# A pooling kernel that streams 168 MB: 840 columns moved into a first piece on 120 partitions, and the last sums done by pairwise adds

## The chip, the cores and the metric

The kernel runs on one core of one Trainium2 chip. The metric is the device time of one execution in microseconds. A run counts as fast when it is within 1.5% of the fastest of the same kernel.

## The reference

The input is 32 x 256 x 4096 fp32, p is 2 and the window is 4. Every four neighbours along the last axis become one output.

```python
window = np.abs(x[:, :, start:end]) ** p
result[:, :, i] = (np.mean(window, axis=-1)) ** (1.0 / p)
```

So each output is the root of a quarter of a sum of four squares. 134.22 MB are read and 33.55 MB are written, and every element is touched once.

## The kernel before

The flat input is treated as 128 partitions of 262,144 columns. SyncE issues the loads, most of them 13,184 columns wide, into three rotating input tiles. ScalarE squares in place, VectorE sums groups of four with a reduce, ScalarE takes the root one chunk later, and ScalarE issues a store for every two loads. The last four stores are issued by SyncE, behind all loads.

```python
    W, O_W = 13184, 6592
    X_SLOTS, O_SLOTS = 3, 2
    slots = [[(W, [4416, 4384, 4384])]] * 18
    slots += [[(6592, [3296, 3296])] * 2, [(6592, [3296, 3296]), (5056, [2528, 2528])]]
    groups = [2] * 9 + [3, 1]
    late = {7, 8, 9, 10}
    # ... cut ...
        for step in chunks:
            v = xs[i][:, c:c + step]
            nc.scalar.activation(out=v, in_=v, func=Act.Square)
            o = ots[g][:, at + c // k:at + (c + step) // k]
            nc.vector.tensor_reduce(
                out=o, in_=v.rearrange("p (n j) -> p n j", j=k),
                axis=mybir.AxisListType.X, op=mybir.AluOpType.add,
            )
            if pending is not None:
                root(*pending)
            # ... cut ...
    root(*pending)
    for g in sorted(late):
        store(g, nc.sync)
```

Of the kernel before, what the change touches and what calls it, by code (L numbers as in the profile page):

```python
# [1 line left out]

# [4 lines left out]


@with_exitstack
def kernel(  # L10
    ctx: ExitStack,
    tc: tile.TileContext,
    x: bass.AP,
    p: float,
    kernel_size: int,
    out: bass.AP,
):






    nc = tc.nc

    assert float(p) == 2.0, "kernel specialized for p == 2"
    k = int(kernel_size)
    assert k == 4, "kernel specialized for kernel_size == 4"

    P = nc.NUM_PARTITIONS  # L30
    fp32 = mybir.dt.float32
    Act = mybir.ActivationFunctionType
    xf = x.rearrange("b c l -> (b c l)")
    of = out.rearrange("b c l -> (b c l)")
    total = xf.shape[0] // P

    W, O_W = 13184, 6592
    X_SLOTS, O_SLOTS = 3, 2
    slots = [[(W, [4416, 4384, 4384])]] * 18
    slots += [[(6592, [3296, 3296])] * 2, [(6592, [3296, 3296]), (5056, [2528, 2528])]]  # L40
    groups = [2] * 9 + [3, 1]
    late = {7, 8, 9, 10}
    in_x = {9, 10}


    loads = [(s, sum(w for w, _ in slot[:j]), *slot[j]) for s, slot in enumerate(slots)
             for j in range(len(slot))]
    n = len(loads)
    assert sum(w for _, _, w, _ in loads) == total

    firsts = [sum(groups[:g]) for g in range(len(groups))]
    assert sum(groups) == n
    group_of = [g for g, count in enumerate(groups) for _ in range(count)]
    columns = [sum(w for _, _, w, _ in loads[firsts[g]:firsts[g] + groups[g]])
               for g in range(len(groups))]

    x_pool = ctx.enter_context(tc.tile_pool(name="x_pool", bufs=X_SLOTS))
    o_pool = ctx.enter_context(tc.tile_pool(name="o_pool", bufs=O_SLOTS))
    ctx.enter_context(tc.manual_schedule())

    def block(flat, g, div):
        at, width = sum(columns[:g]) * P // div, columns[g] * P // div
        return flat[at:at + width].rearrange("(p w) -> p w", p=P)

    slot_tiles = {}
    xs = {}

    def load(i):
        s, at, w, _ = loads[i]
        if at == 0:  # L70
            slot_tiles[s] = x_pool.tile([P, W], fp32, name="xt")
        v = slot_tiles[s][:, at:at + w]
        g = group_of[i]
        src = sum(loads[j][2] for j in range(firsts[g], i))
        nc.sync.dma_start(out=v, in_=block(xf, g, 1)[:, src:src + w])  # L75
        xs[i] = v

    ots = {}

    def store(g, queue):  # L80
        queue.dma_start(out=block(of, g, k), in_=ots[g])  # L81

    def root(g, o, ends):
        nc.scalar.activation(out=o, in_=o, func=Act.Sqrt, scale=1.0 / k)  # L84
        if ends and g not in late:
            store(g, nc.scalar)

    ahead = 0
    while ahead < n and loads[ahead][0] < X_SLOTS - 1:
        load(ahead)  # L90
        ahead += 1
    pending = None
    for i in range(n):
        s, _, w, chunks = loads[i]
        while ahead < n and loads[ahead][0] < s + X_SLOTS:
            load(ahead)
            ahead += 1
        g = group_of[i]
        if i == firsts[g]:
            pool, width = (o_pool, O_W) if g not in in_x else (x_pool, W)  # L100
            t = pool.tile([P, width], fp32, name="ot" if g not in in_x else "xt")
            ots[g] = t[:, 0:columns[g] // k]
        at = sum(loads[j][2] for j in range(firsts[g], i)) // k
        assert sum(chunks) == w
        c = 0
        for step in chunks:
            v = xs[i][:, c:c + step]
            nc.scalar.activation(out=v, in_=v, func=Act.Square)  # L108
            o = ots[g][:, at + c // k:at + (c + step) // k]
            nc.vector.tensor_reduce(  # L110
                out=o, in_=v.rearrange("p (n j) -> p n j", j=k),
                axis=mybir.AxisListType.X, op=mybir.AluOpType.add,
            )
            if pending is not None:
                root(*pending)
            c += step
            pending = (g, o, i == firsts[g] + groups[g] - 1 and c == w)
    root(*pending)
    for g in sorted(late):
        store(g, nc.sync)  # L120


# [1 line left out]
_INS = ['x', 'p', 'kernel_size']  # L124
_OUTS = [((32, 256, 1024), 'float32')]

_NUMBERS = {'p': 2.0, 'kernel_size': 4}


# [26 lines left out]
```

## Time and profile before

| what | value |
|---|---|
| time, median of the first three runs | 394.69 us (394.66 to 394.81) |
| span of the profiled run | 393.0 us |
| VectorE and ScalarE busy | 282.4 and 292.4 us |
| packets of the two data queues | 99.3% of sixteen DMA engines' span |
| last root begins, last store lands, end of the span | 386.42, 392.2, 393.0 us |

The prediction below shows the lines that carry this.

The trace records every DMA packet with its start, duration, size and queue, but not the engine. A packet is here one partition's row of a transfer: 13,184 columns of 4 bytes are 52,736 bytes. An engine's packets can still be chained, because each one starts 4 ns before the recorded end of the one before it. The *excess* is the sum over the 52,736-byte packets of their duration beyond the usual 1947 ns, divided by 16. *Lateness* is how long after the median one the last of the sixteen parts of a transfer lands (the page counts 528 packets under 512 bytes, all of 4 bytes in the records: sixteen for each of the 33 transfers). The *dip* is the stretch of slow packets when the first large store starts.

### The profile page before, as it was taken

To read this page: it belongs to the slowest core of one execution; us is meant where nothing else is said; L and a number is where in the kernel's file an instruction comes from. 1 tells how busy PE (TensorE), PEld (TensorE's weight loads), DVE (VectorE), ACT (ScalarE), POOL (GpSimd) and SP (SyncE) were. 2 spreads that over 40 slices of the span, in tenths; PEclk is the share of its full clock that TensorE was granted. 3 is DMA by queue.
4 is the path that set the end of the run, shared out by engine and by line. 5 is a ranking of instruction groups with operands and counts; after the bars stand their busy time and mean duration, and the time that the engine had idled before them with its cause. 6 is when DMAs were issued, how large, how long until landed. Compare 5 with 4: busy or idle time off the path is not lost.

```text
span 393.0 us, 316 instructions
## 1 busy us (share of the span) xinstructions
DVE 282.4 (72%) x62; ACT 292.4 (74%) x126; POOL 0.2 (0%) x4
## 2 busy tenths in 40 slices
DVE  0068989494959495949594959595859686899992
ACT  1099986777786768686958695959595949899991
POOL 0000000000000000000000000000000000000000
DMA  8999999999999999999999999999999999999997
GB/s 344 429 429 440 429 424 381 443 459 429 413 440 435 429 427 432 429 440 441 437 448 421 432 462 435 392 429 472 429 413 451 425 429 429 424 429 427 438 429 329
DMA packets 4754, 167.79 MB, mean 427 GB/s; under 512 B 528, under 2 KB 528, under 8 KB 656
## 3 DMA queue, kind: packets, MB, share of 16 engines
q1 hardware_dynamic: 3744, 144.15, 85.3%
q10 hardware_dynamic: 1008, 23.63, 14.0%
q14 instruction: 2, 0.02, 0.0%
HBM read 134.22 MB, written 33.55 MB: 427 GB/s over the span
## 4 chain that ended last, share of the span: by engine, by line
DMA 62%; ACT 19%; DVE 14%; issue 2%; ACTq 0%; SPq 0%
DMA xt<-in_x_dram 62%; ACT xt L108 15%; DVE ot L110 11%; DVE xt L110 3%; ACT ot L84 3%; ACT xt L84 1%; ACTq L81 0%; SPq L75 0%; ACTq L108 0%
## 5 line engine op out<-in xcount | busy, mean ns | idle before, releaser
L110 DVE TENSOR_REDUCE ot<-xt 128x1096 f32<-128x4384 f32 (+1 forms) x54 | 255.4, 4731 | 102.7 <-ACT xt L108 102.4
L108 ACT ACTIVATE xt<-xt 128x4384 f32<-128x4384 f32 (+3 forms) x62 | 230.3, 3716 | 89.2 <-DMA xt<-in_x_dram 86.3
L84 ACT ACTIVATE ot<-ot 128x1096 f32<-128x1096 f32 (+1 forms) x54 | 59.8, 1108 | 1.8 <-DVE ot L110 0.9
L110 DVE TENSOR_REDUCE xt<-xt 128x824 f32<-128x3296 f32 (+1 forms) x8 | 27.0, 3384 | 1.3 <-ACT xt L108 1.2
L84 ACT ACTIVATE xt<-xt 128x824 f32<-128x824 f32 (+1 forms) x8 | 6.7, 841 | 3.0 <-DVE xt L110 2.9
L108 ACT ACT_TABLE_LOAD x1 | 1.3, 1283 | 0.7 <-PEq L137 0.7
L84 ACT ACT_TABLE_LOAD x1 | 1.3, 1283 | 0.0
L137 POOL MEMSET const-bfloat16-1.0<- 128x1 bf16 x1 | 0.1, 101 | 0.0
L137 POOL MEMSET const-uint8-127<- 128x1 uint8 x1 | 0.1, 101 | 0.0
L137 POOL MEMSET const-float32-0.0<- 128x1 f32 x1 | 0.1, 98 | 0.2 <-issue 0.2
L137 POOL MEMSET const-float32-1.0<- 128x1 f32 x1 | 0.1, 98 | 0.0
## 6 DMA issues: line engine op xcount, KB each, us to landing
xt<-in_x_dram SPq DMA_DIRECT2D x18, 6592.0 KB, 39.7
out_dram<-ot ACTq DMA_DIRECT2D x7, 3296.0 KB, 26.4
xt<-in_x_dram SPq DMA_DIRECT2D x3, 3296.0 KB, 24.6
out_dram<-ot SPq DMA_DIRECT2D x2, 3296.0 KB, 29.6
xt<-in_x_dram SPq DMA_DIRECT2D x1, 2528.0 KB, 26.4
out_dram<-xt SPq DMA_DIRECT2D x1, 2472.0 KB, 9.3
out_dram<-xt SPq DMA_DIRECT2D x1, 632.0 KB, 5.0
```

Source lines behind the costliest of these rows:

```text
L84: nc.scalar.activation(out=o, in_=o, func=Act.Sqrt, scale=1.0 / k)
L108: nc.scalar.activation(out=v, in_=v, func=Act.Square)
L110: nc.vector.tensor_reduce(out=o, in_=v.rearrange("p (n j) -> p n j", j=k), axis=mybir.AxisListType.X, op=mybir.AluOpType.add,)
L137: nc = _bacc.Bacc("TRN2", target_bir_lowering=False, num_devices=1)
```

## The change

It has two parts. 840 columns are taken from the last load and laid as 120 rows of 896 floats, with a load, a square, a reduce, a root and a store of their own, ahead of everything else. From the seventeenth load on, two adds (first two pairwise sums of each four, then their sum) take the place of the reduce. The rotating tiles also become fixed ones.

```diff
-    slots += [[(6592, [3296, 3296])] * 2, [(6592, [3296, 3296]), (5056, [2528, 2528])]]
+    slots += [[(6592, [3296, 3296])] * 2, [(6592, [3296, 3296]), (4216, [2112, 2104])]]
+    ODD = 840
 ... cut ...
+    PAIRS = 16
 ... cut ...
+        q = v.rearrange("p (n j) -> p n j", j=k)
+        front = v[:, 0:v.shape[1] // 2]
+        h = front.rearrange("p (n j) -> p n j", j=2)
+        nc.vector.tensor_tensor(out=h, in0=q[:, :, 0:2], in1=q[:, :, 2:4], op=add)
+        nc.vector.tensor_tensor(out=o, in0=h[:, :, 0], in1=h[:, :, 1], op=add)
 ... cut ...
+    Q = 120
+    odd = ODD * P // Q
+    t = o_tiles[1][0:Q, 0:odd]
+    nc.sync.dma_start(out=t, in_=xf[(total - ODD) * P:total * P].rearrange("(p w) -> p w", p=Q))
     ahead = 0
 ... cut: the loads of the first three slots ...
+    nc.scalar.activation(out=t, in_=t, func=Act.Square)
+    o = o_tiles[1][0:Q, odd:odd + odd // k]
 ... cut: its reduce ...
+    nc.scalar.activation(out=o, in_=o, func=Act.Sqrt, scale=1.0 / k)
+    nc.scalar.dma_start(
+        out=of[(total - ODD) * P // k:total * P // k].rearrange("(p w) -> p w", p=Q), in_=o,
+    )
```

120 rows look like a wish to use fifteen DMA engines and to spare one for 1.24 us of work. The adds should shorten the compute after the last load.

More of the change, by code (lines that the diff above doesn't have):

```diff
@@ L39 @@
     slots = [[(W, [4416, 4384, 4384])]] * 18
-    slots += [[(6592, [3296, 3296])] * 2, [(6592, [3296, 3296]), (5056, [2528, 2528])]]
+    slots += [[(6592, [3296, 3296])] * 2, [(6592, [3296, 3296]), (4216, [2112, 2104])]]
+    ODD = 840
     groups = [2] * 9 + [3, 1]
     late = {7, 8, 9, 10}
-    in_x = {9, 10}
+    in_x = {9: (2, 0), 10: (2, 4944)}
+    FINE, ENDS, LAG = range(22), (), 1
+    PAIRS = 16
     loads = [(s, sum(w for w, _ in slot[:j]), *slot[j]) for s, slot in enumerate(slots)
@@ L48 @@
     n = len(loads)
-    assert sum(w for _, _, w, _ in loads) == total
+    assert sum(w for _, _, w, _ in loads) + ODD == total
     firsts = [sum(groups[:g]) for g in range(len(groups))]
@@ L55 @@
                for g in range(len(groups))]
-    x_pool = ctx.enter_context(tc.tile_pool(name="x_pool", bufs=X_SLOTS))
-    o_pool = ctx.enter_context(tc.tile_pool(name="o_pool", bufs=O_SLOTS))
+    x_pool = ctx.enter_context(tc.tile_pool(name="x_pool", bufs=1))
+    o_pool = ctx.enter_context(tc.tile_pool(name="o_pool", bufs=1))
+    x_tiles = [x_pool.tile([P, W], fp32, name=f"xt{j}") for j in range(X_SLOTS)]
+    o_tiles = [o_pool.tile([P, O_W], fp32, name=f"ot{j}") for j in range(O_SLOTS)]
     ctx.enter_context(tc.manual_schedule())
@@ L63, in block @@
         return flat[at:at + width].rearrange("(p w) -> p w", p=P)
-    slot_tiles = {}
     xs = {}
@@ L69, in load @@
         s, at, w, _ = loads[i]
-        if at == 0:
-            slot_tiles[s] = x_pool.tile([P, W], fp32, name="xt")
-        v = slot_tiles[s][:, at:at + w]
+        v = x_tiles[s % X_SLOTS][:, at:at + w]
         g = group_of[i]
@@ L86, in root, with total_sum @@
             store(g, nc.scalar)
+    def total_sum(o, v, i):
+        add = mybir.AluOpType.add
+        if i < PAIRS:
+            nc.vector.tensor_reduce(
+                out=o, in_=v.rearrange("p (n j) -> p n j", j=k),
+                axis=mybir.AxisListType.X, op=add,
+            )
+            return
+        q = v.rearrange("p (n j) -> p n j", j=k)
[7 more added lines that the diff above has]
+    nc.sync.dma_start(out=t, in_=xf[(total - ODD) * P:total * P].rearrange("(p w) -> p w", p=Q))
     ahead = 0
-    while ahead < n and loads[ahead][0] < X_SLOTS - 1:
+    while ahead < n and loads[ahead][0] < X_SLOTS:
         load(ahead)
         ahead += 1
-    pending = None
+    nc.scalar.activation(out=t, in_=t, func=Act.Square)
+    o = o_tiles[1][0:Q, odd:odd + odd // k]
+    nc.vector.tensor_reduce(
+        out=o, in_=t.rearrange("p (n j) -> p n j", j=k),
+        axis=mybir.AxisListType.X, op=mybir.AluOpType.add,
+    )
+    nc.scalar.activation(out=o, in_=o, func=Act.Sqrt, scale=1.0 / k)
+    nc.scalar.dma_start(
+        out=of[(total - ODD) * P // k:total * P // k].rearrange("(p w) -> p w", p=Q), in_=o,
+    )
+    pending = []
+    done = 0
     for i in range(n):
@@ L99 @@
         if i == firsts[g]:
-            pool, width = (o_pool, O_W) if g not in in_x else (x_pool, W)
-            t = pool.tile([P, width], fp32, name="ot" if g not in in_x else "xt")
-            ots[g] = t[:, 0:columns[g] // k]
-        at = sum(loads[j][2] for j in range(firsts[g], i)) // k
+            t, first = (o_tiles[g % O_SLOTS], 0) if g not in in_x else (x_tiles[in_x[g][0]], in_x[g][1])
+            ots[g] = t[:, first:first + columns[g] // k]
+            summed = rooted = 0
         assert sum(chunks) == w
@@ L108 @@
             nc.scalar.activation(out=v, in_=v, func=Act.Square)
-            o = ots[g][:, at + c // k:at + (c + step) // k]
-            nc.vector.tensor_reduce(
-                out=o, in_=v.rearrange("p (n j) -> p n j", j=k),
-                axis=mybir.AxisListType.X, op=mybir.AluOpType.add,
-            )
-            if pending is not None:
-                root(*pending)
-            c += step
-            pending = (g, o, i == firsts[g] + groups[g] - 1 and c == w)
-    root(*pending)
+            total_sum(ots[g][:, summed:summed + step // k], v, i)
+            while pending and pending[0][0] <= done - LAG:
+                root(*pending.pop(0)[1:])
+            done += 1
+            c += step
+            summed += step // k
+            ends = summed == columns[g] // k
+            if ends or i in FINE or (i in ENDS and c == w):
+                pending.append((done - 1, g, ots[g][:, rooted:summed], ends))
+                rooted = summed
+    for job in pending:
+        root(*job[1:])
     for g in sorted(late):
```

## The prediction

> **What bounds the kernel now.** I read the page first (busy shares, slices, queues), then the chain of waits, then a table of windows, and at the end the single DMA packets that the trace records.
>
> ```profile
> span 393.0 us, 316 instructions
> DVE 282.4 (72%) x62; ACT 292.4 (74%) x126; POOL 0.2 (0%) x4
> DMA  8999999999999999999999999999999999999997
> ...
> q1 hardware_dynamic: 3744, 144.15, 85.3%
> q10 hardware_dynamic: 1008, 23.63, 14.0%
> ```
>
> No compute engine is full, but the DMA row is at 9 in every slice but the first and the last, and the packets of the two data queues take 85.3 + 14.0 = 99.3% of sixteen engines' span. That leaves 0.7% of 393 us, 2.75 us, idle per engine. The window table tells where (columns: window, length, DVE busy, ACT busy, POOL busy, clock, DMA share, GB/s):
>
> ```profile
> 0.00:1.70 1.70, 0.00 (x0) 0.98 (x1) 0.20 (x4) 1.00 0.00 0
> 1.70:4.00 2.30, 0.00 (x0) 0.31 (x1) 0.00 (x0) 1.00 1.13 367
> 4.00:40.00 36.00, 15.09 (x4) 19.69 (x9) 0.00 (x0) 1.00 1.03 444
> 40.00:56.00 16.00, 14.60 (x4) 14.50 (x6) 0.00 (x0) 1.00 0.99 422
> 56.00:62.00 6.00, 5.44 (x2) 5.96 (x3) 0.00 (x0) 1.00 0.94 334
> 62.00:70.00 8.00, 7.36 (x2) 3.77 (x2) 0.00 (x0) 1.00 0.99 428
> 70.00:383.00 313.00, 236.95 (x52) 245.31 (x105) 0.00 (x0) 1.00 1.00 433
> ```
>
> Nothing moves for 1.7 us (the first load is issued at 0.73 us), then 433 GB/s nearly to the end. The one dip is 334 GB/s at 56 to 62 us, when the first output store, issued by ScalarE at 55.62 us, starts. It costs (433 - 334) x 6 us = 594 KB, or 1.4 us.
>
> The chain of waits could mislead (shares by engine):
>
> ```profile
> DMA 62%; ACT 19%; DVE 14%; issue 2%; ACTq 0%; SPq 0%
> ```
>
> and its last pieces, in order of time (start, length, what):
>
> ```profile
> 380.48 0.89 ACT xt L84
> 381.37 2.21 ACT xt L108
> 383.57 0.02 issue
> 383.60 2.80 DVE xt L110
> 386.39 0.02 issue
> 386.42 0.73 ACT xt L84
> ```
>
> It ends with square (L108), sum (L110), root (L84), and then the last store. From 339.7 us on, ScalarE is nearly full. Does that tail hold the end? The last store is issued at 387.15 us; issue to first packet was 1.0 us for the first load (0.73 to 1.74), so its packets could have begun at about 388.2. The packet records show them beginning at 389.2, each engine's following the 19,776-byte packets of the store before almost without a gap. So the tail has about 1.0 us of slack, and the DMA engines set the time: the last packet ends at 391.71, lands at 392.2, and the kernel ends at 393.0.
>
> Packet costs, from the same records: 52,736 bytes take 1947 ns, 26,368 take 978, 5,056 take 194. The line through the first two is 9 ns + 0.03675 ns per byte and gives 195 for the third. In undisturbed packets one engine's sixteenth is (2304 x 1947 + 1536 x 978 + 128 x (754 + 735 + 194)) / 16 ns = 387.7 us; 1.9 us to begin, about 0.65 us of slow first packets and some 1.3 us of slow packets near the first store make 391.5. Fifteen engines start their first packet between 1.74 and 2.28 us, one not before 3.19, so about 1.25 us late. At the end it (or whichever is last) is only 0.145 us behind the next (391.71 against 391.57): in this run the other engines lost their lead in the dip.
>
> [...]
>
> **The change part by part.**
>
> 1. Small piece, DMA engines. 840 columns leave the last 128-row load and store and come as 120 rows of 896 floats. Bytes are the same in total. Taken away per engine: 8 rows x (3360 + 840 bytes) x 0.03675 ns = 1.24 us. Added on fifteen engines: 8 x (9 + 3584 x 0.03675) = 1.13 us for the load and 8 x (9 + 896 x 0.03675) = 0.34 us for the store. Net +0.23 us on fifteen engines, -1.24 us on the spared one. That 1.24 equals the late engine's 1.25 us is surely the intent. I take the spared engine to be the late one; the trace does not number them. The kernel ends with its latest engine, now the next in line: -0.145 + 0.23 = +0.09 us.
>
> 2. Small piece, first use of the store queue. A 430 KB load landing near 4.5 us, its square (0.93 us[...]), reduce (1.09), a table load (1.28, under the reduce) and root (0.37) put the first ScalarE-issued store at about 7 us, on fifteen engines, instead of at 55.6. If the dip of 1.4 us belongs to the first use of that queue, it moves there; with only 107 KB it may shrink. If it belongs to the first large store, it stays. I give shrinking some 35% and about 1 us of gain: -0.35 us in the mean.
>
> 3. First loads. Three slots are asked for at once instead of two and one more directly after: before, the third was already issued ahead of any wait, so nothing moves. The small load delays the large ones by one issue (about 0.4 us), under which fifteen engines have 1.13 us of small rows: 0, or +0.1 on the spared engine.
>
> 4. Pairwise adds from load 16 on: 14 reduces become 28 adds. For 4384 columns [...]3.74 us replaces 4.72; for 3296, 2.89 replaces 3.59; for the last chunk (2104, was 2528), 1.96 replaces 2.78. VectorE loses 6 x 0.98 + 6 x 0.70 + 2 x 0.82 = 11.7 us of busy time. On the tail's path the gain is smaller, as ScalarE paces it: its waits of 0.94 and 0.67 us for VectorE go, the last two squares lose 0.35 us each, two roots 0.1 each, the last sum 0.84: 3.3 us. The last store is issued at about 384 instead of 387.15. All of it goes into slack, which grows from 1.0 to about 4 us, because the engines are still busy with the store before.
>
> 5. Fixed tiles in place of rotating ones, output groups 9 and 10 together in the third input tile: the instruction order of the SyncE loads and stores is otherwise the same, slots are reused as before, and I see no new wait. 0.
>
> Sum: +0.09 - 0.35 + 0.05 = -0.2 us. I predict **394.4 us**, after adding a further -0.1 for unprofiled runs in which the late engine may trail by more than the 0.145 us of this one profile.
>
> **Rivals.** (a) *The tail is the bound*: then part 4 gives 2 to 3 us, about 392 us. For it: the chain ends there, ScalarE is full from 339.7. Against it: the last store's packets queue behind others without a gap. (b) *The late engine is the bound and the dip shrinks*: the dip is what hid its lateness. If it shrinks, the ordinary engines end near 390.7 and sparing the late one is worth its whole 1.2 us: about 393.4. For it: the equality of 1.24 and 1.25. Against it: nothing shows that the dip depends on a first use. (c) *The small piece hurts*: small packets, or a wrong engine spared (the late one then carries +0.23), or a second dip: 394.9 to 396. (d) *The adds are slower[...]*, as the strided reads might make them: if they took twice as long, 5.8 us per 3296 columns against ScalarE's 3.7, VectorE would pace the tail and ten microseconds would be added. [...]I give this 1%.
>
> **Range and chances.** The terms are tenths of a microsecond, and repeats differ by 0.15 us; (b) and (c) span 393.4 to 395. Eight in ten: 393.2 to 395.1. Two per cent is 7.9 us, more than all idle time of the DMA engines (2.75 us) and the dip (1.4 us) together, so faster by over 2% is out of reach; slower needs rival (d).
>
> **What would show it.** Right: adds near 1.87 and 1.02 us for 3296 columns; VectorE's busy time about 10.6 us lower (11.7 less the small reduce); the last root near 384 us and yet the last landing within 1 us of 392.2; DMA share at 1.00 through the tail; the small load and store in fifteen parts. Wrong: DMA slices under 9 in the middle (a new wait for a slot), a dip at 56 to 62 us gone or doubled, a last store whose packets begin only after a gap, or a start later than 1.74 us.

The sum has lost no term: +0.09 - 0.35 + 0.05 is -0.21 us, and with the further -0.1 the 394.69 us of the kernel before become 394.4. But two of its grounds only the changed kernel's trace shows:

- *Fifteen engines, eight rows each*, on which the +0.09 rests. No transfer of 120 rows was in the trace before, whose 33 transfers of 128 rows have 528 packets of 4 bytes, sixteen each. The changed kernel has two transfers more and 558, fifteen for each of the two; the fifteen chains of the small load are described below.
- *The costs of the single instructions.* The adds for 4384, 3296 and 2104 columns took 2442 + 1300, 1875 + 1016 and 1255 + 707 ns, the 3.74, 2.89 and 1.96 us of the fourth point. The small piece's square, reduce, table load and root took 0.95, 1.09, 1.28 and 0.39 us.

The trace before did show that loads and stores take turns on an engine: beside the first large store (55.6 us on), a chain of packets goes 52,736 bytes, 26,368, 52,736, 26,368. Its stores take 26.2 us in the median to land and 33.7 at most, although none has more than 3.4 MB, about 8 us at 433 GB/s.

## More of the kernel before

The part of the page on DMA issues adds how the tail is built; its columns are the transfer, its issuer, the count, the size and the median time from issue to landing.

```profile
out_dram<-ot SPq DMA_DIRECT2D x2, 3296.0 KB, 29.6
xt<-in_x_dram SPq DMA_DIRECT2D x1, 2528.0 KB, 26.4
out_dram<-xt SPq DMA_DIRECT2D x1, 2472.0 KB, 9.3
out_dram<-xt SPq DMA_DIRECT2D x1, 632.0 KB, 5.0
```

The last store has only 632 KB and yet needs 5.0 us, because it stands behind the 2472 KB one, whose last packets end at 390.18 us.

## The result and the profile after

The median is 394.60 us (394.56 to 394.93, six runs), against 394.87 us for the kernel before in its six runs. The ratio of the fast runs is 0.9996, with a 95% interval of 0.9983 to 1.0008: the same time. A ratio is the mean time of one kernel's fast runs over the mean of the other's from the same rounds, so it is not quite the ratio of the medians quoted.

These are the page's lines of the changed kernel that answer to those of before: the span, the busy times, the DMA row in 40 slices, and the data queues.

```profile
span 392.8 us, 341 instructions
DVE 271.8 (69%) x77; ACT 292.5 (74%) x128; POOL 0.2 (0%) x4
DMA  9999999999999989999999999999999999999997
...
q1 hardware_dynamic: 3879, 144.04, 85.2%
q10 hardware_dynamic: 1143, 23.73, 14.0%
```

VectorE has 10.6 us less to do, and the span is 0.2 us shorter. The DMA engines are as full as before.

The beginning, from the timeline (start, length, engine, line, what, and the idle time before it):

```profile
0.73 0.46 SPq L112 DMA_DIRECT2D ot<-in_x_dram  x1
1.24 53.43 SPq L80 DMA_DIRECT2D xt<-in_x_dram  x5
4.74 0.95 ACT L117 ACTIVATE ot<-ot 120x896 f32<-120x896 f32 x1 [2.73 <-DMA ot<-in_x_dram]
7.42 0.64 ACTq L124 DMA_DIRECT2D out_dram<-ot  x1
20.36 7.63 ACT L143 ACTIVATE xt<-xt 128x4416 f32<-128x4416 f32 x2 [12.97 <-DMA xt<-in_x_dram]
```

The small piece is computed by 7.4 us, but the first large tile is squared at 20.36 us instead of 19.53, and the last full tile at 340.62 instead of 339.75. These are the two lines of the kernel before, and then the last full tile of the changed one:

```profile
19.53 7.63 ACT L108 ACTIVATE xt<-xt 128x4416 f32<-128x4416 f32 x2 [17.52 <-DMA xt<-in_x_dram]
339.75 3.88 ACT L108 ACTIVATE xt<-xt 128x4416 f32<-128x4416 f32 x1 [1.07 <-DMA xt<-in_x_dram]
```

```profile
340.62 3.88 ACT L143 ACTIVATE xt<-xt 128x4416 f32<-128x4416 f32 x1 [1.19 <-DMA xt<-in_x_dram]
```

What was put in front of the stream pushed the whole stream back.

The end of the tail, from the same view:

```profile
380.26 4.88 SPq L86 DMA_DIRECT2D out_dram<-xt  x2
...
382.12 1.25 DVE L105 TENSOR_TENSOR xt<-xt 128x1052 f32<-128x1052 f32 x1 [0.95 <-ACT xt L143]
383.41 0.71 DVE L106 TENSOR_TENSOR xt<-xt 128x526 f32<-128x526 f32 x1
384.15 0.64 ACT L89 ACTIVATE xt<-xt 128x526 f32<-128x526 f32 x1 [1.53 <-DVE xt L106]
```

The last root begins at 384.15 us instead of 386.42, and the last packet still ends at 391.41 (391.71 before). The time from issue to landing of that store rises accordingly: it carries 527 KB and takes longer than the 632 KB one took.

```profile
out_dram<-xt SPq DMA_DIRECT2D x1, 527.0 KB, 7.1
```

The reduce of the kernel before and the adds, from the groups with shapes kept apart (line, engine, operation, shapes, count, busy time, mean ns of one):

```profile
L110 DVE TENSOR_REDUCE xt<-xt 128x824 f32<-128x3296 f32 x6 | 21.5, 3586 | 0.9 <-ACT xt L108 0.7
```

```profile
L105 DVE TENSOR_TENSOR xt<-xt 128x1648 f32<-128x1648 f32 x6 | 11.3, 1875 | 3.9 <-ACT xt L143 3.8
L106 DVE TENSOR_TENSOR xt<-xt 128x824 f32<-128x824 f32 x6 | 6.1, 1016 | 0.2
```

1875 + 1016 ns replace 3586 ns for 3296 columns, 2.89 us for 3.59, as the prediction has it.

One reading needs care. These are the windows of the changed kernel around the first large store, with the columns of the prediction's table:

```profile
56.00:62.00 6.00, 5.45 (x2) 5.55 (x4) 0.00 (x0) 1.00 1.20 488
62.00:70.00 8.00, 7.96 (x2) 4.64 (x2) 0.00 (x0) 1.00 0.86 369
70.00:383.00 313.00, 227.40 (x67) 245.28 (x106) 0.00 (x0) 1.00 1.00 433
```

A DMA share of 1.20 is impossible as a measure of work in a window. Packets of 52 KB on sixteen engines that run nearly in step are booked whole into one window or its neighbour, and sixteen of them are 844 KB. So windows of a few microseconds say nothing about tenths of a microsecond here. The packet durations do. Between 55 and 66 us their excess is 0.99 us per engine before and 0.43 us after.

### The profile page after: what moved, and what is told of

Read it like the earlier page. It is cut to its first block, busy times and chain, and to the rows that moved or that the text cites. A ratio compares the mean times of both kernels' runs of the same rounds, so it can differ in the third digit from the quotient of the medians.

```text
span 392.8 us, 341 instructions
## 1 busy us (share of the span) xinstructions
DVE 271.8 (69%) x77; ACT 292.5 (74%) x128; POOL 0.2 (0%) x4
## 4 chain that ended last, share of the span: by engine, by line
DMA 62%; ACT 21%; DVE 10%; issue 4%; SPq 0%; ACTq 0%
DMA xt<-in_x_dram 62%; ACT xt L143 17%; DVE ot L96 8%; ACT ot L89 3%; ACT xt L89 1%; DVE xt L105 1%; DVE xt L106 0%; ACTq L86 0%; SPq L80 0%; SPq L112 0%; ACTq L89 0%
## 5 line engine op out<-in xcount | busy, mean ns | idle before, releaser
L143 ACT ACTIVATE xt<-xt 128x4384 f32<-128x4384 f32 (+4 forms) x62 | 229.6, 3705 | 85.1 <-DMA xt<-in_x_dram 81.9
L96 DVE TENSOR_REDUCE ot<-xt 128x1096 f32<-128x4384 f32 (+1 forms) x48 | 227.0, 4731 | 90.1 <-ACT xt L143 89.8
L105 DVE TENSOR_TENSOR xt<-xt 128x1648 f32<-128x1648 f32 (+4 forms) x14 | 28.4, 2032 | 16.0 <-ACT xt L143 16.0
L89 ACT ACTIVATE xt<-xt 128x824 f32<-128x824 f32 (+2 forms) x8 | 6.5, 817 | 1.9 <-DVE xt L106 1.9
L106 DVE TENSOR_TENSOR ot<-xt 128x1096 f32<-128x1096 f32 (+1 forms) x6 | 7.8, 1303 | 0.2
L106 DVE TENSOR_TENSOR xt<-xt 128x824 f32<-128x824 f32 (+2 forms) x8 | 7.5, 939 | 0.3
L119 DVE TENSOR_REDUCE ot<-ot 120x224 f32<-120x896 f32 x1 | 1.1, 1086 | 5.7 <-ACT ot L117 5.7
L117 ACT ACTIVATE ot<-ot 120x896 f32<-120x896 f32 x1 | 0.9, 949 | 2.7 <-DMA ot<-in_x_dram 2.7
## 6 DMA issues: line engine op xcount, KB each, us to landing
out_dram<-xt SPq DMA_DIRECT2D x1, 2472.0 KB, 10.4
```

What stands on the lines that cost most here:

```text
L89: nc.scalar.activation(out=o, in_=o, func=Act.Sqrt, scale=1.0 / k)
L96: nc.vector.tensor_reduce(out=o, in_=v.rearrange("p (n j) -> p n j", j=k), axis=mybir.AxisListType.X, op=add,)
L105: nc.vector.tensor_tensor(out=h, in0=q[:, :, 0:2], in1=q[:, :, 2:4], op=add)
L106: nc.vector.tensor_tensor(out=o, in0=h[:, :, 0], in1=h[:, :, 1], op=add)
L117: nc.scalar.activation(out=t, in_=t, func=Act.Square)
L119: nc.vector.tensor_reduce(out=o, in_=t.rearrange("p (n j) -> p n j", j=k), axis=mybir.AxisListType.X, op=mybir.AluOpType.add,)
```

## The experiments

The theory: the DMA engines' bytes set the time, so the adds only buy slack (time by which the compute may end later at no cost), and the small piece moves at most tenths. The rivals: the compute tail holds the end; the spared engine is worth 1.2 us; an early first store shrinks the dip. Twelve kernels ran, on three chips. The kernel before had medians of 394.94, 394.86 and 394.75 us beside them, in this order. All results were correct.

### A second trace of the kernel before

No edit.

> The kernel before, unchanged, for a second trace. Theory (DMA-bound, the slow packets near the first large store are its own): excess over the usual 1947 ns of the 52,736-byte packets again about 2.0 us per engine, 1.25 us of it between 35 and 65 us; one engine begins its first packet about 1.2 us after the others; last packet ends near 391.7 us. Rival (the dip is chance): the excess differs by more than half a microsecond between the two traces of one kernel, and the last packet moves with it.

Measured: 394.82 us. The excess is 2.02 us per engine in all, as in the first trace, 1.19 of it between 55 and 66 us (0.99 in the first), and the last packet ends at 391.61. So the dip belongs to the kernel. The late engine does not belong to it in the same way: in this trace the last of the sixteen engines begins at 2.51 us, not at 3.19, and in the trace of the adds alone, below, at 3.48. The 1.25 us to which I fitted the 1.24 us of spared work was one draw.

### Each part alone

The small piece without the adds (it keeps the fixed tiles):

```diff
-    PAIRS = 16
+    PAIRS = 22
```

> The small piece without the pairwise adds (all sums are reduces again). Theory: the adds only buy slack in the tail; last root ends near 386.5 us, time equal to the changed kernel, 394.6 within 0.2. Rival (the tail holds the end): 1 to 2 us slower than the changed kernel.

The adds without the small piece (in the kernel before):

```diff
-            nc.vector.tensor_reduce(
... cut: its arguments ...
+            if i < 16:
+                nc.vector.tensor_reduce(
... cut: the same arguments ...
+            else:
+                q = v.rearrange("p (n j) -> p n j", j=k)
+                h = v[:, 0:step // 2].rearrange("p (n j) -> p n j", j=2)
+                nc.vector.tensor_tensor(out=h, in0=q[:, :, 0:2], in1=q[:, :, 2:4], op=mybir.AluOpType.add)
+                nc.vector.tensor_tensor(out=o, in0=h[:, :, 0], in1=h[:, :, 1], op=mybir.AluOpType.add)
```

> The kernel before with the pairwise adds from load 16 on, no small piece. Theory: last root near 384.5 us instead of 387.15, time equal to the kernel before within 0.2 us. Rival (the tail holds the end): 1 to 3 us faster than the kernel before.

Measured: the small piece alone takes 394.62 us (ratio to before 0.9992, interval 0.9978 to 1.0006), its last root begins at 386.42. The adds alone take 394.92 us (0.9999, 0.9986 to 1.0011), with the last root at 384.02. In this order:

```profile
386.42 0.64 ACT L89 ACTIVATE xt<-xt 128x526 f32<-128x526 f32 x1 [1.88 <-DVE xt L96]
```

```profile
384.02 0.73 ACT L84 ACTIVATE xt<-xt 128x632 f32<-128x632 f32 x1 [1.77 <-DVE xt L119]
```

Over two microseconds of earlier compute leave the time where it was, in both pairs (394.62 against 394.60, 394.94 against 394.92). The adds contribute nothing to the time. If the change gains the 0.3 us at all, the small piece does (or the fixed tiles, but the next run keeps those, and its last packet is back at 391.58 us).

### The small piece on 128 partitions

```diff
-    Q = 120
+    Q = 128
```

> The small piece on 128 partitions, so that all sixteen engines share it; all else as in the changed kernel. If the 0.3 us that the last packet came earlier is due to the spared engine: back to about 394.9, the late engine again among the last. If it is due to the earlier first store (a smaller dip at 56 to 65 us): 394.6 as in the changed kernel and the dip's excess near 0.4 us per engine.

Measured: 394.78 us (ratio to before 1.0000, 0.9988 to 1.0013), the last packet at 391.58, the excess at the first large store 1.08. Here sixteen engines share an early store as small as that of the change (its page counts 561 packets under 512 bytes; 35 transfers of sixteen parts make 560), and the dip is as deep as before. So the early first use of the store queue is not what makes it small; the rival that I had given 35% falls. With 120 rows the excess is 0.43, 0.36 (the small piece alone) and 0.24 us (the tail probe below); with the piece on 128 rows, or without one, it is between 0.65 and 1.21 us in six traces.

### Does sparing an engine help? Five times the piece

```diff
-    slots += [... (4216, [2112, 2104])]]
-    ODD = 840
+    slots += [... (856, [428, 428])]]
+    ODD = 4200
```

It ran with Q at 120, 128 and 112.

> Five times the small piece (4200 columns) on 120 partitions. If a 120-row transfer runs on fifteen engines and spares the one that begins late: that engine ends some 6.2 us before the others (it has 168 KB less, at 0.03675 ns per byte), the others carry 11.2 KB more, 0.41 us, so the time is 0.2 to 0.5 us above the changed kernel. If it runs on sixteen: all engines end together and the time does not move.

> The same 4200 columns on 128 partitions, the control for the run on 120. All sixteen engines carry the same; 0.2 to 0.5 us faster than the run on 120 partitions if sparing one engine costs the others, equal otherwise.

> The large piece on 112 rows: sixteen engines with seven rows each[...]. On 120 rows (fifteen engines, eight rows each) a packet of 17,920 bytes took 1381 ns, on 128 rows one of 16,800 took 626. If it is the unequal number of engines that slows the 120 rows: about 715 ns for the 19,200-byte packets here and a time near 396. If it is that the rows are not cut as in a 128-row transfer: about 1400 ns and a time near 400.

Measured: 400.73, 396.09 and 398.51 us (the last a single look, its state unknown). All three are slower, as far as a single look can tell it of the last, and the first by over ten times the loss that I expected. The windows from 4 to 20 us, on 120, 128 and 112 rows in turn, show where:

```profile
4.00:20.00 16.00, 1.70 (x1) 5.22 (x2) 0.00 (x0) 1.00 1.00 313
```

```profile
4.00:20.00 16.00, 4.53 (x1) 6.06 (x3) 0.00 (x0) 1.00 1.06 458
```

```profile
4.00:20.00 16.00, 3.62 (x1) 5.49 (x2) 0.00 (x0) 1.00 1.01 358
```

On 120 rows the engines are busy all the time (share 1.00) and move 313 GB/s. Their packets of 17,920 bytes take 1381 ns in the median, where the 9 ns + 0.03675 ns per byte of the other packets gives 668. On 128 rows a packet of 16,800 bytes takes 626 ns, as that line gives. On 112 rows one of 19,200 bytes takes 1185 ns instead of 715. I have no count of the engines for these 112 rows; my estimate from the bytes of the windows is sixteen, seven rows each. In the first 20 us (158 GB/s up to 4 us, 358 after) 6.36 MB moved, the piece's 2.15 MB and 80 large packets, five for each of sixteen engines; fourteen engines with eight rows each would leave two free for nine, some 88 in all. So these loads on fewer than 128 rows are slow row by row, with fifteen engines and, by that estimate, with sixteen; then it is not the number of engines. The stores of the same pieces are not slow: 4480 bytes on 120 rows took 173 ns, as the line gives, and 896 bytes in the changed kernel's trace, where they take turns with 52,736-byte loads, took 41 in the median (42 by the line). In the change the same happens on a smaller scale: the median packet of 3584 bytes takes 160 ns instead of 141, a quarter of them more than 233, and the small load costs an engine 1.64 us instead of the 1.13 I added up. Most of this is not the rows: the first packets are slow without them too, and on 128 rows, where the median packet of 3360 bytes takes 132 ns as the line gives, the small load costs 1.48 us instead of 1.06. But the large packets beside them are slower as well. Over all packets that begin before 5 us, the time beyond the line is 0.86 us per engine with 120 rows, 0.53 with 128 and 0.65 in the kernel before.

Why rows that are cut otherwise than in 128 are slow, no run here shows.

Fifteen engines it is: in the changed kernel's trace fifteen chains begin with eight 3584-byte packets each at 1.75 to 2.15 us, and one begins at about 2.96 us with a large one. (The landings say the same: one of the sixteen counts of the small load comes at 1.30 us, before any packet, the other fifteen from 3.80 us on.) This spared engine can only begin with the second load, which is issued 0.5 us after the first. Its 1.24 us less work is spent on its late start. At the end one engine trails as it did: the last part of the last store lands 0.71 us after the median in the changed kernel, 0.86 with the small piece alone, 0.70 with the piece on 128 rows, and 0.60, 0.51 and 1.07 in the three traces without a small piece. Sparing an engine did not shorten the end.

The run on 128 rows also lost 1.2 us, for another reason. The 4200 columns in front push the last full tile's square from 340.62 to 346.06 us, so the compute tail no longer fits:

```profile
385.00:386.60 1.60, 0.68 (x3) 1.31 (x3) 0.00 (x0) 1.00 0.29 124
386.60:388.60 2.00, 0.24 (x1) 0.29 (x1) 0.00 (x0) 1.00 0.90 376
```

The share of 0.29 is a real hole, about 2 us wide in the chains of most engines. The store before the last is issued at 385.70 us, 5.4 us later than in the changed kernel, and the engines have run dry.

### How much slack has the tail?

An idle square ahead of the last root, on data no longer needed. In the changed kernel:

```diff
+    idle = x_tiles[0][:, 0:8768]
+    nc.scalar.activation(out=idle, in_=idle, func=Act.Square)
     for job in pending:
```

> The changed kernel with the same idle instruction ahead of its last root, which delays the last store's issue by about 5.9 us to 390.7. Theory (slack 3.3 us): 2.3 to 2.9 us slower than the changed kernel. Rival (no slack): 5.9 us slower.

Measured: 396.14 us. The timeline has the root 5.76 us later than the 384.15 of the change:

```profile
382.51 7.49 ACT L155 ACTIVATE xt<-xt 128x8768 f32<-128x8768 f32 x1
383.39 0.71 DVE L106 TENSOR_TENSOR xt<-xt 128x526 f32<-128x526 f32 x1
389.91 0.62 ACT L89 ACTIVATE xt<-xt 128x526 f32<-128x526 f32 x1
```

5.76 us of delay cost 1.54 us (396.14 - 394.60), less than the 2.3 to 2.9 that I expected. If every microsecond beyond the slack costs one, 4.2 us were slack.

The same square in the kernel before, on the tile of slot 18, failed as a probe:

> The kernel before with one idle ScalarE instruction of 8768 columns (about 7.5 us, on data no longer needed) ahead of the last root, which delays the last store's issue by about 5.3 us to 392.4. Theory (1.0 us of slack in the tail): 4 to 4.5 us slower than the kernel before. Rival (no slack, the tail is the bound): 5.3 us slower. Rival (much slack): under 3 us.

Measured: 407.79 us, 12.9 us slower instead of about 4. The timeline tells why:

```profile
390.69 5.48 DVE L110 TENSOR_REDUCE xt<-xt 128x632 f32<-128x2528 f32 x2 [10.35 <-DMA out_dram<-xt]
```

VectorE waits 10.35 us for a store. My square used a rotating tile after its last real use, which lengthened that tile's life, and the last output group got a buffer that was being stored. The probe measured its own wait. The mended one squares a chunk in place, three times, where no tile lives longer:

```diff
+    idle = xs[n - 1][:, 0:2528]
+    for _ in range(3):
+        nc.scalar.activation(out=idle, in_=idle, func=Act.Square)
     root(*pending)
```

> The probe of the kernel before once more, mended: three idle squares of 2528 columns, in place on the last chunk but one, which is already summed, so that no tile's lifetime changes. They end near 390.9 us, so the last root ends near 391.6 and the last store is issued about 4.5 us later than the 387.15 of the kernel before. Theory (2.0 us of slack, counted as in the changed kernel's probe, where 5.7 us of delay cost 1.5): 2.2 to 3.2 us slower than the kernel before. Rival (the tail is the bound): 4.5 us slower.

Measured: 397.27 us.

```profile
384.18 6.98 ACT L120 ACTIVATE xt<-xt 128x2528 f32<-128x2528 f32 x3
391.06 0.71 ACT L84 ACTIVATE xt<-xt 128x632 f32<-128x632 f32 x1
```

4.64 us of delay (391.06 against 386.42) cost 2.52 us (397.27 - 394.75), as expected, so 2.1 us were slack. The change lifted the slack from 2.1 to 4.2 us. That is what the adds are: an insurance that this kernel did not need.

### What makes the dip small?

My new theory was that the dip at the first large store is deep when all engines run in step. An extra load of eight rows on top of the piece on 128 rows should put half of the engines half a packet behind. I took it that the rows go to eight engines, one each, and hold these up by the 0.98 us that a packet of 26,368 bytes takes in the kernel before; no run here shows on how many engines eight rows move:

```diff
-    Q = 120
+    Q = 128
 ... cut ...
+    nc.sync.dma_start(out=o_tiles[0][0:8, 0:6592], in_=xf[0:8 * 6592].rearrange("(p w) -> p w", p=8))
     ahead = 0
```

> The small piece on 128 partitions, and behind it one extra load of 8 rows of 26,368 bytes into a tile that is not yet in use[...]. Theory (the dip at the first large store is deep when all engines are in step; spread-out starts make it small): excess between 55 and 66 us at most 0.5 us per engine, against 1.08 with the small piece on 128 partitions alone; [...]the time is 0.2 to 0.7 us longer than that run's 394.8. Rival (fewer than sixteen engines in the early store make the dip small): excess about 1.1, time 0.8 to 1.1 us longer.

And as a candidate without added bytes, 240 columns as eight rows:

```diff
-    slots += [... (4216, [2112, 2104])]]
-    ODD = 840
+    slots += [... (4816, [2416, 2400])]]
+    ODD = 240
-    Q = 120
+    Q = 8
```

> A candidate: 240 columns as 8 rows of 3840 floats in place of 840 on 120 rows. No byte is added[...]. Theory (spreading the engines makes the dip small): excess between 55 and 66 us 0.3 to 0.7 us per engine, time 394.4 to 394.9. Rival: excess about 1.1, time 395.0 to 395.3.

Measured: the excess at the first large store falls to 0.02 and 0.13 us, the second lower than expected. The times are 397.33 and 395.33 us, both worse than expected. In the first run the eight packets of 26,368 bytes take 2.57 us in the median instead of 0.98, so this eight-row load is slow itself, and the large packets up to 35 us have 1.6 us of excess per engine, against 0.7 in the kernel before. In the candidate these have 1.2 us. Its packets of 15,360 bytes take 942 ns in the median instead of 573, but they are the first of the run, and first packets are slow on 128 rows too (those of the large piece there take 1.45 us in the median instead of 0.63), so they do not show that eight rows are slow.

And the theory does not hold against the other traces. I counted how many engines begin a packet within the same half microsecond, some 8 us before the first large store. In the tail probe of the changed kernel it is all sixteen, and its excess is 0.24. In the kernel before it is eleven, and its excess is 0.99. Being in step is not the cause.

One thing does go with the dip in all fourteen traces, once the window follows the store. With 4200 columns in front, the first large store is issued at 62.17 us on 128 rows (55.62 in the kernel before), and a window that ends at 66 us cuts its dip off. Taken from 0.6 us before the issue to 10.4 after it, the excess there is 0.65 us, and on 120 and 112 rows it is still 0.01. So the seven traces without a load on fewer than 128 rows have 0.65 to 1.21 us, and the seven with one have 0.01 to 0.43. The two go together, but no run shows what links a slow load at 2 to 13 us to a store some 50 us later. The cause of the dip stays open, and so does the reason why it shrinks with 120 rows.

No run was faster than the kernel before beyond the intervals, and none had a lower median than the change, so there is no better version to report.

## Why the prediction was right

The forecast was 394.4 us within 393.2 to 395.1, the same time with 98%; the result is 394.60. Step by step:

- **The bound.** Right. The DMA rows before and after are full, and each part alone leaves the time as it was. The rival that the tail is the bound fell with the two probes.
- **Slack in the tail, "about 1.0 us" growing "to about 4".** The direction was right and the first size wrong: 2.1 us measured before, 4.2 after. I had measured only up to the first packet of the last store, but the engines come free one after the other, from 389.20 to 390.18 us, and the store's packets fill the gaps.
- **The adds.** Right, 1875 and 1016 ns, and 10.6 us less on VectorE. The 3.3 us of a shorter tail path are there too: 340.62 to 384.15 is 43.53 us, 339.75 to 386.42 is 46.67, a difference of 3.14, and the last root itself is 0.09 us shorter. But the last root came only 2.27 us earlier. The step that failed is in the third point of the change, which counted the small load in front as "0, or +0.1": it pushed the last full tile 0.87 us back. It cost slack and no time.
- **Net +0.23 us on fifteen engines.** Too small. The small load took 1.64 us per engine instead of 1.13, but slow first packets make up most of that (1.48 instead of 1.06 on 128 rows), and the kernel before has them on its large ones. What the sum took for granted is that rows on 120 partitions move as fast as on 128: with them the packets up to 5 us lose 0.86 us against the line, with 128 rows 0.53.
- **The spared engine is the late one.** Not shown. The lateness of the first packets changes from trace to trace (3.19, 2.51, 3.48 us), and the final lateness of 0.5 to 1.1 us is there with and without sparing.
- **A smaller dip, -0.35 us in the mean.** The gain came, 0.56 us per engine (0.99 to 0.43), but not for the reason given: the run on 128 rows has the early store and the full dip. Its size, 1.4 us, was read from a window of six microseconds; the packets from 55 to 66 us give 0.99.
- **The sum.** In the trace the packets of an engine take 389.40 us after and 389.84 before. A smaller dip outweighs the slower small load, the last packet ends 0.30 us earlier and the median is 0.27 us lower. The interval of the ratio contains 1, so even these tenths rest on the traces. What was right is that the DMA engines set the time and the tail does not; that the tenths of the sum also came out near is luck, because its largest term came, but not for the reason given.

## What to carry to other kernels

When sixteen DMA engines are full from the first load to the last store, ask of every change how many bytes and packets it takes off the busiest engine; compute that ends earlier only lengthens the queue in front of it (here the last store took 7.1 us to land instead of 5.0). Measure slack by delaying the thing and seeing what the delay costs, and make sure that the probe does not lengthen a tile's life. Don't fit a piece of work to a lateness of one trace, and let a window follow the event that it measures. Keep loads on all 128 partitions: here a row of the large piece cost 1.7 to 2.1 times as much on 112 and 120.
